# Two transformer blocks on one core: where the row sums of the conditioning products are issued, which engine does half of a norm's first pass, the root's steps, and when a norm's parameters are loaded

## The chip, the core and the metric

The kernel runs on one core of a Trainium2 chip. The engines of a core work side by side, each on a queue of its own in order: TensorE (PE in the profile, with PEld for its weight loads), VectorE (DVE), ScalarE (ACT), GpSimd (POOL) and SyncE (SP), whose queue issues nearly all DMA transfers. They wait for one another by semaphores. The metric is the device time of one execution in microseconds (us); lower is better.

## What is computed

256 tokens of width 1024 pass through a first block of two layers (with a memory of 256 tokens) and then through a second block of two layers, whose norms are modulated by a conditioning vector. Cut to what matters here:

```python
def layer_norm(x, g, b):
    xf = x.astype(jnp.float32)
    mu = jnp.mean(xf, axis=-1, keepdims=True)
    var = jnp.mean(jnp.square(xf - mu), axis=-1, keepdims=True)
    y = (xf - mu) * lax.rsqrt(var + LN_EPS) * g.astype(jnp.float32) + b.astype(jnp.float32)
    return y.astype(x.dtype)
...
    for l in range(DEPTH):
        x = layer_norm(DN_ALPHA * x + 0.5 * swiglu_ffn(x, ffn_w_in[l, 0], ffn_w_out[l, 0]),
                       ln_g[l, 0], ln_b[l, 0])
        x = layer_norm(DN_ALPHA * x + mixer_sublayer(x, w_mix_in[l], b_gate[l], kv_norm_g[l], w_uk[l],
...
        x = layer_norm(DN_ALPHA * x + memory_cross_attention(x, mem, xa_wq[l], xa_wkv[l], xa_wo[l]),
                       ln_g[l, 2], ln_b[l, 2])
        x = layer_norm(DN_ALPHA * x + 0.5 * swiglu_ffn(x, ffn_w_in[l, 1], ffn_w_out[l, 1]),
                       ln_g[l, 3], ln_b[l, 3])
...
def rms_norm_2(x, g):
    xf = x.astype(jnp.float32)
    y = xf * lax.rsqrt(jnp.mean(xf * xf, axis=-1, keepdims=True) + EPS)
    return (y * g.astype(jnp.float32)).astype(x.dtype)
...
def adaln(cond, mod_w, mod_b):
    return jnp.split(jax.nn.silu(cond) @ mod_w + mod_b, 6, axis=-1)

def modulate(h, shift, scale):
    return h * (1 + scale) + shift
```

The second block's layers add a gated mixer (even: two kinds of attention with a context stream beside the tokens; odd: neighbourhood attention) and a gated swiglu with d_ff 2816. Shift, scale and gate, six vectors of 1024 for each layer, come from `adaln`.

## The kernel before

**Matrix products.** Weights are loaded in fp32 as tiles of 128 x 1024 (`wf`, three buffers, 512 KB each) by SP. Each is split into a high part `wh` by a cast on ACT (L199) and a low part `wl` by a subtraction on DVE (L200); the activations are split in the same way. A product is then three matmuls on PE, L204 to L206. This fills PE for nearly the whole span, with DVE and ACT feeding it.

**The ends of stages.** The first block has four stages in each layer: `ffn_in` and `ffn_out`, `mixer`, `cross`, and a second pair `ffn_in` and `ffn_out`. Each ends in `post_ln`, which calls `layer_norm` for each half of the tokens (tb 0 and 1): L295 adds the accumulators from PSUM to the residual with its row sum, ACT squares, L302 gives the negated mean `nm`, L305 does the first pass (subtract the mean, multiply by g) on the first 512 columns and L313 on the second 512, L308 gives the variance `ve`, `rsqrt` (L248 to L260) the inverse root, and L314 does the last pass (multiply by the root, add b) on each half. Then PE transposes the result (L277) and the next stage begins. Its parameters g and b are two tiles of 512 KB, loaded by `ln_params` in `post_ln`, behind the loads of the stage in front. The kernel has eight such ends, and 16 calls of `layer_norm`.

**The root.** `rsqrt` begins with an integer operation on the bits (L248) and takes three Newton steps. For one value per partition (n = 1) a step has two operations, L256 and L260. For n > 1 there are ten in all. The second block's norms call it too (`modulating`, whose scaled activations are L970, and the norms of heads).

**The conditioning products.** `adaln` is a generator. It computes shift, scale and gate as 160 row sums on DVE (L911, a multiplication of a `wa` tile of 128 x 1024 with the conditioning vector, with accumulation). A `wa` tile has 512 KB and one buffer; the load of the next one is issued behind the last product that reads it. For layer 0 and the first two kinds of layer 1 a tile serves two products, for the other four kinds of layer 1 one. Whoever calls `mods(n)` pulls n products: the units of `ffn_in` from the third on (in the very first `ffn_in` from the eleventh on), and each unit of `ffn_out`. `until(thirds)` pulls all that are missing for a third of a layer's kinds: it stands behind the even attention (3), behind the `ffn_in` of the second block's first layer (4) and behind the odd attention (6), ahead of the output projection and of `gated`.

**The end of the odd attention.** The last heads' maxima (L462, L463), the splits of the output (L200), then the projection by `w2_out` (`projS`), `gated` (L1000 multiplies the accumulators by the gate, L1001 adds the residual), then the norm ahead of the last ffn (L964, L965, `rsqrt`, L970), whose transposes are PE's next work.

**What sets the order.** A scheduler of the framework orders each engine's instructions when the program is built, from the order of the code and the buffers; `self.held` keeps the first weight splits of the next stage behind the norm's last pass.

Of the kernel before, what the change touches and what calls it, by code (L numbers as in the profile page):

```python
# [25 lines left out]
FT = DFF // P  # L26
# [10 lines left out]
RSQRT_SCALE = 2.0 ** (-13 / 27)  # L37
RSQRT_SEED = 1597463007.0 + round(-13 / 27 * 2 ** 23) - 2.0 ** 31
# [67 lines left out]
class Net:  # L106
# [136 lines left out]
    def rsqrt(self, v, n):  # L243
# [9 lines left out]
        for i in range(3):  # L253
            a = self.t([P, 32], "ra", 2)[:, :n]
            if n == 1:
                V.scalar_tensor_tensor(a, y, v, y, ALU.mult, ALU.mult)  # L256
            else:
                V.tensor_tensor(a, y, z, ALU.mult)
            y2 = self.t([P, 32], "rq", 6)[:, :n]
            V.scalar_tensor_tensor(y2, a, 3 * s * s, y, ALU.subtract, ALU.mult)  # L260
            if n > 1 and i < 2:
                z2 = self.t([P, 32], "rq", 6)[:, :n]
                V.scalar_tensor_tensor(z2, a, 3 * s * s, z, ALU.subtract, ALU.mult)
                z = z2
            y = y2
            s = 2 * s ** 3
# [14 lines left out]
    def layer_norm(self, x, tb, acc, scale, gb, eps, xs, after):  # L281
# [23 lines left out]
        V.scalar_tensor_tensor(y[:, halves[0]], r[:, halves[0]], nm, gb[0][:, halves[0]], ALU.add, ALU.mult)  # L305
        jk = self.t([P, 3], "jd", 2)
# [4 lines left out]
        for i, s in enumerate(halves):  # L311
            if i == 1:
                V.scalar_tensor_tensor(y[:, s], r[:, s], nm, gb[0][:, s], ALU.add, ALU.mult)  # L313
# [29 lines left out]
    def post_ln(self, acc, x, scale, l, i, eps, want_xs=True):  # L343

        gb = self.ln_params(l, i)
# [9 lines left out]
    def ffn_in(self, src, streams, between=None):  # L355
# [20 lines left out]
        for j in range(2, FT):  # L376
            w = self.weight(src[j], UNIT)
            if not between or j > 9:
                self.mods(n)
# [28 lines left out]
    def projB(self, src, n, nk, part, amid=iter(()), done=()):  # L408
# [6 lines left out]
        for u in range(nu):  # L415
# [3 lines left out]
            if nk == FT:  # L419
# [409 lines left out]
    def first_block(self, dbg=None, depth=DEPTH):  # L829
# [19 lines left out]
        for l in range(depth):  # L849
            g = self.ffn_in(I["ffn_w_inA"][l, 0], [xs], between if l == 0 else None)  # L850
            if l == 0:
                self.constants()
                x = [self.k4() for _ in range(NT)]
                for tb in range(NT):
                    self.load(x[tb], I["xN"][:, tb])
            (acc,) = self.ffn_out(I["ffn_w_outB"][l, 0], 1, g)
            xs = self.post_ln(acc, x, 2 * ALPHA, l, 0, 4 * LN_EPS)
            if dbg: dbg(f"x{l}0", x)
            acc = self.mixer(l, xs)
            self.mem_kv(l)  # L860
            xs = self.post_ln(acc, x, ALPHA, l, 1, LN_EPS)
            if dbg: dbg(f"x{l}1", x)
            acc = self.cross(l, xs)
            xs = self.post_ln(acc, x, ALPHA, l, 2, LN_EPS)
            if dbg: dbg(f"x{l}2", x)
            g = self.ffn_in(I["ffn_w_inA"][l, 1], [xs])
            (acc,) = self.ffn_out(I["ffn_w_outB"][l, 1], 1, g, self.second_params() if l == DEPTH - 1 else iter(()))
            xs = self.post_ln(acc, x, 2 * ALPHA, l, 3, 4 * LN_EPS, want_xs=l < DEPTH - 1)
# [748 lines left out]
```

## Time and profile before

| | before |
|---|---|
| median of 3 runs | 2552.11 us (2548.66 to 2557.58) |
| the profiled execution | 2549.47 us, of which the span is 2547.7 |
| granted clock of TensorE, mean | 0.984 |
| PE busy | 96% of the span |
| DVE busy | 65% |
| ACT busy | 46% |
| GpSimd busy | 3% |
| products L911 | 160, 193.6 us |

A page gives each engine's busy time, the groups of instructions with their mean duration, and the idle time of an engine with what ended it. In a timeline row the first number is the start, the second the time the instruction (or a run of x such) took, and the brackets hold the idle time before it and what ended that. A tile's name stands for its class of buffers: `k` are the working tiles, `pa` and `pj` the PSUM accumulators, `wf`, `wh`, `wl` the weights, `wa` the conditioning weights.

### The profile page before, as it was taken

Reading aid. Unit: us, or ns where it says so; the run is one execution under the profiler, and the core shown is the slowest. Engines: PE = TensorE matmul, PEld = TensorE weight load, DVE = VectorE, ACT = ScalarE, POOL = GpSimd, SP = SyncE. Lnnn points to the kernel's source line nnn. Section 1 sums busy time; section 2 is a strip of 40 time slices with the busy share of each in tenths; the row PEclk is TensorE's granted clock in tenths of the full one; section 3 lists DMA queues with packets and bytes.
Section 4 is the critical chain, followed back from the end, with each engine's and each line's share of the span. In section 5 each row is a group of like instructions: output and inputs, shape, how many; then the busy total and the mean of one; then the engine's idle time right before and its main releaser. Section 6 shows DMA issues by size and latency. Waiting matters only on the chain.

```text
span 2547.7 us, 39416 instructions
## 1 busy us (share of the span) xinstructions
PE 2442.3 (96%) x15166; PEld 2138.6 (84%) x15166; DVE 1660.2 (65%) x3325; ACT 1177.6 (46%) x1948; POOL 68.7 (3%) x88
## 2 busy tenths in 40 slices
PE   8998999989999999999899999899999999998999
PEld 8987989869979979999789877677888887776997
DVE  6566776577667667766677776776554537646654
ACT  5444464454444444555444545654222324555542
POOL 0000100000000000100000000000000000032000
PEclk9999999999999999999999999999999999999999
DMA  7774535547757755446447642013455632342554
GB/s 260 232 245 163 163 116 184 184 140 242 243 178 249 235 188 179 142 143 208 167 170 241 226 161 70 31 42 109 158 188 192 214 102 91 110 99 74 182 191 140
DMA packets 138844, 423.64 MB, mean 166 GB/s; under 512 B 29128, under 2 KB 36000, under 8 KB 138528
## 3 DMA queue, kind: packets, MB, share of 16 engines
q1 hardware_dynamic: 138656, 421.12, 50.8%
q8 instruction: 119, 1.95, 0.3%
q14 instruction: 69, 0.57, 0.1%
HBM read 416.84 MB, written 4.23 MB: 165 GB/s over the span
## 4 chain that ended last, share of the span: by engine, by line
PE 77%; DVE 12%; DMA 5%; ACT 3%; issue 2%; POOL 0%; SPq 0%; POOLq 0%; ACTq 0%; DVEq 0%
PE pj L204 17%; PE pj L206 17%; PE pj L205 17%; PE pa L205 7%; PE pa L204 7%; PE pa L206 6%; DVE wl L200 3%; PE pa L277 3%; DMA k<-in_rpbF_dram 1%; DMA wf<-in_ffn_w_outB_dram 1%; DVE mx L462 1%; ACT wh L199 1%; DVE k L200 1%; ACT a L465 1%; DMA wf<-in_mix_A_dram 1%
## 5 line engine op out<-in xcount | busy, mean ns | idle before, releaser
L199 ACT CAST wh<-wf 128x1024 fp32r<-128x1024 f32 (+2 forms) x652 | 673.0, 1034 | 938.5 <-PE pj L205 232.0
L200 DVE TENSOR_TENSOR wl<-wf,wh 128x1024 fp32r<-128x1024 f32 (+2 forms) x652 | 783.8, 1207 | 452.7 <-PE pj L206 130.4
L204 PE MATMUL pj<-k,wh 128*128 128x256 f32 (+1 forms) x2896 | 841.6, 291 | 0.0
L205 PE MATMUL pj<-k,wh 128*128 128x256 f32 (+1 forms) x2896 | 838.6, 290 | 0.0
L206 PE MATMUL pj<-k,wl 128*128 128x256 f32 (+1 forms) x2896 | 838.4, 290 | 0.0
L204 PEld LDWEIGHTS pj<-k,wh 128*128 128x128 f32 x2896 | 554.6, 192 | 14.4 <-issue 7.1
L205 PEld LDWEIGHTS pj<-k,wh 128*128 128x128 f32 x2896 | 554.3, 191 | 8.5 <-issue 1.3
L206 PEld LDWEIGHTS pj<-k,wl 128*128 128x128 f32 x2896 | 554.3, 191 | 7.5 <-issue 0.7
L204 PE MATMUL pa<-wh,k 128*128 128x512 f32 x688 | 272.3, 396 | 2.4 <-ACT k L199 2.4
L205 PE MATMUL pa<-wl,k 128*128 128x512 f32 x688 | 274.2, 398 | 0.4 <-DVE wl L200 0.2
L204 PE MATMUL pj<-wh,k 128*128 128x512 f32 (+1 forms) x616 | 250.2, 408 | 12.5 <-ACT wh L199 7.3
L205 PE MATMUL pj<-wl,k 128*128 128x512 f32 (+1 forms) x616 | 249.6, 405 | 3.1 <-DVE wl L200 2.9
L911 DVE SCALAR_TENSOR_TENSOR k<-wa,cond 128x1024 bf16<-128x1024 f32 x160 | 193.6, 1222 | 83.5 <-DMA wa<-in_mod_wT_dram 83.2
L206 PE MATMUL pa<-wh,a 128*128 128x512 f32 x560 | 218.0, 390 | 0.0
L206 PE MATMUL pj<-wh,k 128*128 128x512 f32 (+1 forms) x496 | 199.8, 403 | 2.9 <-DVE k L200 2.9
L204 PEld LDWEIGHTS pa<-wh,k 128*128 128x128 f32 x688 | 129.0, 187 | 36.2 <-ACT k L199 3.5
L204 PEld LDWEIGHTS pj<-wh,k 128*128 128x128 f32 x616 | 119.8, 194 | 40.2 <-ACT wh L199 8.5
L205 PEld LDWEIGHTS pa<-wl,k 128*128 128x128 f32 x688 | 129.2, 188 | 28.7 <-DVE wl L200 1.2
L205 PEld LDWEIGHTS pj<-wl,k 128*128 128x128 f32 x616 | 120.0, 195 | 28.8 <-DVE wl L200 5.1
L277 PE MATMUL pa<-ident,k 128*128 128x128 f32 x580 | 96.5, 299 | 49.3 <-DVE k L314 23.1
L277 PEld LDWEIGHTS pa<-ident,k 128*128 128x128 f32 x580 | 70.7, 152 | 82.5 <-DVE k L314 29.5
L206 PEld LDWEIGHTS pa<-wh,a 128*128 128x128 f32 x560 | 105.4, 188 | 25.3 <-DVE a L200 0.5
(252 smaller groups left out, 2417.4 us busy)
## 6 DMA issues: line engine op xcount, KB each, us to landing
wf<-in_ffn_w_inA_dram SPq DMA_DIRECT2D x262, 512.0 KB, 4.3
wf<-in_ffn_w_outB_dram SPq DMA_DIRECT2D x132, 512.0 KB, 4.4
wf<-in_mix_A_dram SPq DMA_DIRECT2D x108, 512.0 KB, 3.7
wa<-in_mod_wT_dram SPq DMA_DIRECT2D x96, 512.0 KB, 4.3
wf<-in_w_branchA_dram SPq DMA_DIRECT2D x32, 384.0 KB, 3.1
wf<-in_od_w_dram SPq DMA_DIRECT2D x24, 512.0 KB, 3.9
wf<-in_w_mix_outB_dram SPq DMA_DIRECT2D x16, 512.0 KB, 4.7
wf<-in_w_outB_dram SPq DMA_DIRECT2D x16, 512.0 KB, 3.7
```

The lines of the kernel that those rows point to most:

```text
L199: self.nc.scalar.copy(h, x)
L200: self.nc.vector.tensor_tensor(l, x, h.bitcast(F32), ALU.subtract)
L204: mm(ps, sh, mh, start=start, stop=False)
L205: mm(ps, sh, ml, start=False, stop=False)
L206: mm(ps, sl, mh, start=False, stop=stop)
L277: self.nc.tensor.transpose(ps[:, i * P:(i + 1) * P], b, self.ident)
L462: V.reduce_max(mx[:, i:i + 1], ps[:, a:b], axis=AX.X)
L465: nc.scalar.activation(p[:, a:b], ps[:, a:b], AF.Exp, bias=mx[:, i:i + 1], scale=scale, accum_out=sm[:, i:i + 1])
L911: V.scalar_tensor_tensor(junk, w, 1.0, self.cond[:, s], ALU.mult, ALU.mult, accum_out=mod[:, n, s:s + 1])
```

## The change

`ffn_in` pulls products from its sixth unit on (`j > 4`) where it was the third, the very first one as before; `ffn_out` no longer pulls in its last three units. The first pass of the second 512 columns moves from DVE (one scalar_tensor_tensor, L313) to GpSimd (a tensor_scalar and a tensor_tensor). The root takes two steps, the first of a higher order and with an operation more, from another first guess: five operations behind the integer one for n = 1 where there were six. `ln_params` is called ahead of `ffn_out`, of `mem_kv` and of `cross`, and its tiles are handed to `post_ln`. In the changed program lines move: L200 is L201, L305 is L310, L314 is L319, L256 is L257, L260 is L265, L911 is L919, L1000 is L1008; L262 is the new operation of the root's first step.

```diff
@@ -34,8 +34,9 @@
 IDX_SCALE = float(8 ** -0.5 * 64 ** -0.5)
 UNIT = 2048
 
-RSQRT_SCALE = 2.0 ** (-13 / 27)
-RSQRT_SEED = 1597463007.0 + round(-13 / 27 * 2 ** 23) - 2.0 ** 31
+
+RSQRT_SCALE = -(3 / 8 * 2 ** (-1 / 3)) ** (1 / 5)
+RSQRT_SEED = 1597463007.0 + round(math.log2(-RSQRT_SCALE) * 2 ** 23) - 2.0 ** 31
 
 
 class Split:
@@ -250,20 +251,24 @@
         if n > 1:
             z = self.t([P, 32], "rq", 6)[:, :n]
             V.tensor_tensor(z, y, v, ALU.mult)
-        for i in range(3):
+        for i in range(2):
             a = self.t([P, 32], "ra", 2)[:, :n]
             if n == 1:
                 V.scalar_tensor_tensor(a, y, v, y, ALU.mult, ALU.mult)
             else:
                 V.tensor_tensor(a, y, z, ALU.mult)
+            c = -3 * s * s
+            if i == 0:
+                V.scalar_tensor_tensor(a, a, -10 / 3 * s * s, a, ALU.add, ALU.mult)
+                c = 5 * s ** 4
             y2 = self.t([P, 32], "rq", 6)[:, :n]
-            V.scalar_tensor_tensor(y2, a, 3 * s * s, y, ALU.subtract, ALU.mult)
-            if n > 1 and i < 2:
+            V.scalar_tensor_tensor(y2, a, c, y, ALU.add, ALU.mult)
+            if n > 1 and i == 0:
                 z2 = self.t([P, 32], "rq", 6)[:, :n]
-                V.scalar_tensor_tensor(z2, a, 3 * s * s, z, ALU.subtract, ALU.mult)
+                V.scalar_tensor_tensor(z2, a, c, z, ALU.add, ALU.mult)
                 z = z2
             y = y2
-            s = 2 * s ** 3
+            s = 8 / 3 * s ** 5
         return y
 
     def warm(self, func, src):
@@ -303,14 +308,14 @@
         V.tensor_tensor(far, nm, near, ALU.subtract)
         V.scalar_tensor_tensor(ss[:, 2:3], far, -float(D), far, ALU.mult, ALU.mult)
         V.scalar_tensor_tensor(y[:, halves[0]], r[:, halves[0]], nm, gb[0][:, halves[0]], ALU.add, ALU.mult)
+        nc.gpsimd.tensor_scalar(y[:, halves[1]], r[:, halves[1]], nm, 1.0, ALU.add, ALU.mult)
+        nc.gpsimd.tensor_tensor(y[:, halves[1]], y[:, halves[1]], gb[0][:, halves[1]], ALU.mult)
         jk = self.t([P, 3], "jd", 2)
         ve = self.t([P, 1], "ve", 2)
         V.tensor_scalar(jk, ss, 1.0 / D, eps, ALU.mult, ALU.add, accum_out=ve)
         rs = self.rsqrt(ve, 1)
         c = slice(tb * P, (tb + 1) * P)
         for i, s in enumerate(halves):
-            if i == 1:
-                V.scalar_tensor_tensor(y[:, s], r[:, s], nm, gb[0][:, s], ALU.add, ALU.mult)
             z = V.scalar_tensor_tensor(y[:, s], y[:, s], rs, gb[1][:, s], ALU.mult, ALU.add)
             if xs is not None:
                 ps = self.transposes([y[:, (4 * i + k) * P:(4 * i + k + 1) * P] for k in range(4)])
@@ -340,9 +345,8 @@
             self.load(gb[j], self.I[nm][l, i:i + 1, :].broadcast_to((P, D)))
         return gb
 
-    def post_ln(self, acc, x, scale, l, i, eps, want_xs=True):
-
-        gb = self.ln_params(l, i)
+    def post_ln(self, acc, x, scale, gb, eps, want_xs=True):
+
         xs = Split(self, KT) if want_xs else None
         z, zs = None, []
         for tb in range(NT):
@@ -375,7 +379,7 @@
             nc.scalar.copy(at(s, 0)[:, :, tb * P:(tb + 1) * P], pt[:, :256].rearrange("p (j t) -> p j t", j=2))
         for j in range(2, FT):
             w = self.weight(src[j], UNIT)
-            if not between or j > 9:
+            if j > (9 if between else 4):
                 self.mods(n)
             if j % (4 // n) == 0:
                 more()
@@ -416,7 +420,7 @@
             w = self.weight(src[u], UNIT)
             now = [part(i, u) for i in range(n)]
             next(amid, None)
-            if nk == FT:
+            if nk == FT and u < nu - 3:
                 self.mods(n)
             for i in range(n):
                 unit = (*now[i], w)
@@ -853,19 +857,23 @@
                 x = [self.k4() for _ in range(NT)]
                 for tb in range(NT):
                     self.load(x[tb], I["xN"][:, tb])
+            gb = self.ln_params(l, 0)
             (acc,) = self.ffn_out(I["ffn_w_outB"][l, 0], 1, g)
-            xs = self.post_ln(acc, x, 2 * ALPHA, l, 0, 4 * LN_EPS)
+            xs = self.post_ln(acc, x, 2 * ALPHA, gb, 4 * LN_EPS)
             if dbg: dbg(f"x{l}0", x)
             acc = self.mixer(l, xs)
+            gb = self.ln_params(l, 1)
             self.mem_kv(l)
-            xs = self.post_ln(acc, x, ALPHA, l, 1, LN_EPS)
+            xs = self.post_ln(acc, x, ALPHA, gb, LN_EPS)
             if dbg: dbg(f"x{l}1", x)
+            gb = self.ln_params(l, 2)
             acc = self.cross(l, xs)
-            xs = self.post_ln(acc, x, ALPHA, l, 2, LN_EPS)
+            xs = self.post_ln(acc, x, ALPHA, gb, LN_EPS)
             if dbg: dbg(f"x{l}2", x)
             g = self.ffn_in(I["ffn_w_inA"][l, 1], [xs])
+            gb = self.ln_params(l, 3)
             (acc,) = self.ffn_out(I["ffn_w_outB"][l, 1], 1, g, self.second_params() if l == DEPTH - 1 else iter(()))
-            xs = self.post_ln(acc, x, 2 * ALPHA, l, 3, 4 * LN_EPS, want_xs=l < DEPTH - 1)
+            xs = self.post_ln(acc, x, 2 * ALPHA, gb, 4 * LN_EPS, want_xs=l < DEPTH - 1)
             if dbg: dbg(f"x{l}3", x)
         return x
 
```

**Place 1, DVE at the end of the odd attention of the second block.** The rows before, from the last splits of the attention's output (`k` from `pa`) over the low parts of the output projection's weights to the gate:

```order
L200 TENSOR_TENSOR k_4566_22546<-pa_23307,k_4564_22544 128x256
L200 TENSOR_TENSOR k_4566_22546<-pa_23354,k_4564_22544 128x256
L200 TENSOR_TENSOR wl_23464<-wf_23461,wh_23463 128x1024
L200 TENSOR_TENSOR wl_23470<-wf_23467,wh_23469 128x1024
L200 TENSOR_TENSOR wl_23476<-wf_23473,wh_23475 128x1024
L200 TENSOR_TENSOR wl_23637<-wf_23634,wh_23636 128x1024
L1000 TENSOR_TENSOR k_4815_23529<-pa_23379,k_4814_23527 128x512
L1001 TENSOR_TENSOR k_4102_20485<-k_4102_20485,k_4815_23529 128x512
```

The rows now at the same place, up to the gate (L1008 was L1000; six products stand further up, most of them beside the last heads):

```order
L201 TENSOR_TENSOR wl_23238<-wf_23235,wh_23237 128x1024
L201 TENSOR_TENSOR wl_23393<-wf_23390,wh_23392 128x1024
L919 SCALAR_TENSOR_TENSOR k_4609_23098,mod_18996<-wa_23094,cond 128x1024
L919 SCALAR_TENSOR_TENSOR k_4611_23102,mod_18996<-wa_23100,cond 128x1024
L201 TENSOR_TENSOR wl_23399<-wf_23396,wh_23398 128x1024
L919 SCALAR_TENSOR_TENSOR k_4613_23106,mod_18996<-wa_23104,cond 128x1024
L919 SCALAR_TENSOR_TENSOR k_4615_23110,mod_18996<-wa_23108,cond 128x1024
L919 SCALAR_TENSOR_TENSOR k_4617_23114,mod_18996<-wa_23112,cond 128x1024
L919 SCALAR_TENSOR_TENSOR k_4619_23118,mod_18996<-wa_23116,cond 128x1024
L919 SCALAR_TENSOR_TENSOR k_4621_23122,mod_18996<-wa_23120,cond 128x1024
L919 SCALAR_TENSOR_TENSOR k_4623_23126,mod_18996<-wa_23124,cond 128x1024
L1008 TENSOR_TENSOR k_4657_23291<-pa_23141,k_4656_23289 128x512
```

The products of layer 1's last kinds, which had been issued long before, stand between the weights' splits and directly ahead of the gate. Here `wl_23238` is the last split of the output projection's weights, `wl_23393` and `wl_23399` belong to the ffn behind it.

**Place 2, DVE in the first `post_ln`, first half of the tokens.** The rows before, from the mean to the last pass:

```order
L305 SCALAR_TENSOR_TENSOR k_350_2063<-k_216_1523,nm_2074,k_326_2005 128x512
L304 SCALAR_TENSOR_TENSOR ss_2065<-nm_2074 128x1
L313 SCALAR_TENSOR_TENSOR k_350_2063<-k_216_1523,nm_2074,k_326_2005 128x512
L308 TENSOR_SCALAR jd_2079,ve_2080<-ss_2065 128x3
L248 TENSOR_SCALAR rq_2082<-ve_2080 128x1
L256 SCALAR_TENSOR_TENSOR ra_2084<-rq_2082,ve_2080 128x1
L260 SCALAR_TENSOR_TENSOR rq_2086<-ra_2084,rq_2082 128x1
L256 SCALAR_TENSOR_TENSOR ra_2088<-rq_2086,ve_2080 128x1
L260 SCALAR_TENSOR_TENSOR rq_2090<-ra_2088,rq_2086 128x1
L256 SCALAR_TENSOR_TENSOR ra_2092<-rq_2090,ve_2080 128x1
L260 SCALAR_TENSOR_TENSOR rq_2094<-ra_2092,rq_2090 128x1
L314 SCALAR_TENSOR_TENSOR k_350_2063<-k_350_2063,rq_2094,k_327_2006 128x512 x2
```

The rows now:

```order
L310 SCALAR_TENSOR_TENSOR k_343_2051<-k_216_1523,nm_2062,k_217_1526 128x512
L309 SCALAR_TENSOR_TENSOR ss_2053<-nm_2062 128x1
L201 TENSOR_TENSOR wl_2121<-wf_2118,wh_2120 128x1024
L315 TENSOR_SCALAR jd_2069,ve_2070<-ss_2053 128x3
L249 TENSOR_SCALAR rq_2072<-ve_2070 128x1
L257 SCALAR_TENSOR_TENSOR ra_2074<-rq_2072,ve_2070 128x1
L262 SCALAR_TENSOR_TENSOR ra_2074<-ra_2074 128x1
L265 SCALAR_TENSOR_TENSOR rq_2077<-ra_2074,rq_2072 128x1
L257 SCALAR_TENSOR_TENSOR ra_2079<-rq_2077,ve_2070 128x1
L265 SCALAR_TENSOR_TENSOR rq_2081<-ra_2079,rq_2077 128x1
L319 SCALAR_TENSOR_TENSOR k_343_2051<-k_343_2051,rq_2081,k_218_1527 128x512 x2
```

L313 is gone from DVE, the root is one operation shorter, with the square (L262) in its first step, and L310 reads a parameter tile of a lower number.

**Place 3, SP around the end of the first layer's mixer.** The rows before, at the norm's parameters (`xa_q` and `xa_woB` are weights of `cross`):

```order
L159 DMA wf_5567<-in_xa_q_dram 128x1024
L159 DMA wf_5573<-in_xa_q_dram 128x1024
L159 DMA wf_5579<-in_xa_q_dram 128x1024
L159 DMA wf_5711<-in_xa_woB_dram 128x1024
L159 DMA k_961_5451<-in_ln_g_dram 128x1024
L159 DMA k_962_5452<-in_ln_b_dram 128x1024
L159 DMA wf_5717<-in_xa_woB_dram 128x1024
L159 DMA wf_5723<-in_xa_woB_dram 128x1024
```

The rows now, at the same parameters, among the weights of the mixer's output projection:

```order
L160 DMA wf_5008<-in_w_branchA_dram 128x768
L160 DMA wf_5014<-in_w_branchA_dram 128x768
L160 DMA wf_5074<-in_w_mix_outB_dram 128x1024
L160 DMA k_913_5218<-in_ln_g_dram 128x1024
L160 DMA wf_5080<-in_w_mix_outB_dram 128x1024
L160 DMA wf_5110<-in_w_mix_outB_dram 128x1024
L160 DMA k_914_5219<-in_ln_b_dram 128x1024
L160 DMA wf_5116<-in_w_mix_outB_dram 128x1024
L160 DMA wf_5146<-in_w_mix_outB_dram 128x1024
```

The load of g moved from place 212 of SP's queue to place 187, that of b from 213 to 190.

## Rows read from the trace of the kernel before

**Rows 1.** The page's first section: busy us, share, instructions of each engine.

```profile
PE 2442.3 (96%) x15166; PEld 2138.6 (84%) x15166; DVE 1660.2 (65%) x3325; ACT 1177.6 (46%) x1948; POOL 68.7 (3%) x88
```

**Rows 2.** PE's waits: us in total, times, longest.

```profile
PE pa L277 <- DVE k L314: 23.1, 12, 4.5
PE pa L277 <- DVE k L970: 9.7, 3, 3.9
```

**Rows 3.** DVE's waits, the same columns.

```profile
DVE k L305 <- DMA k<-in_ln_g_dram: 13.7, 2, 8.0
```

**Rows 4.** Timeline of DVE and PE at both mixers' ends.

```profile
503.12 0.75 DVE L305 SCALAR_TENSOR_TENSOR k<-k,nm,k 128x512 f32<-128x512 f32 x1 [8.00 <-DMA k<-in_ln_g_dram]
...
505.29 1.97 PE L277 MATMUL pa<-ident,k 128*128 128x128 f32 x8 [4.46 <-DVE k L314]
515.54 1.71 PE L277 MATMUL pa<-ident,k 128*128 128x128 f32 x11 [1.23 <-DVE k L314]
...
1243.48 1.78 PE L277 MATMUL pa<-ident,k 128*128 128x128 f32 x8 [2.13 <-DVE k L314]
1253.54 0.66 PE L277 MATMUL pa<-ident,k 128*128 128x128 f32 x4 [1.70 <-DVE k L314]
```

**Rows 5.** Timeline of the first norm on DVE; two later stage ends on PE.

```profile
199.59 0.22 DVE L256 SCALAR_TENSOR_TENSOR ra<-rq,ve 128x1 f32<-128x1 f32 x1
199.84 0.16 DVE L260 SCALAR_TENSOR_TENSOR rq<-ra,rq 128x1 f32<-128x1 f32 x1
200.03 0.22 DVE L256 SCALAR_TENSOR_TENSOR ra<-rq,ve 128x1 f32<-128x1 f32 x1
200.17 1.22 DVE L200 TENSOR_TENSOR wl<-wf,wh 128x1024 fp32r<-128x1024 f32 x1
...
201.94 1.41 DVE L314 SCALAR_TENSOR_TENSOR k<-k,rq,k 128x512 f32<-128x512 f32 x2
...
757.99 1.69 PE L277 MATMUL pa<-ident,k 128*128 128x128 f32 x10 [3.45 <-DVE k L314]
1500.32 1.94 PE L277 MATMUL pa<-ident,k 128*128 128x128 f32 x8 [3.92 <-DVE k L970]
```

**Rows 6.** Timeline of GpSimd in two stretches, with one split of DVE.

```profile
273.32 1.49 POOL L656 TENSOR_TENSOR a<-k,sc 128x128 f32<-128x128 f32 x1
275.47 0.46 POOL L656 TENSOR_TENSOR a<-k,sc 128x128 f32<-128x128 f32 x1
...
273.27 1.23 DVE L200 TENSOR_TENSOR wl<-wf,wh 128x1024 fp32r<-128x1024 f32 x1 [0.51 <-issue]
...
2281.49 0.69 POOL L1362 TENSOR_SCALAR k<-k,sm 128x512 f32<-128x512 f32 x1
2282.15 1.00 POOL L1341 TENSOR_TENSOR k<-k,a 128x384 f32<-128x384 f32 x1
```

**Rows 7.** The products: all 160, two in a row, SP's issues, landing.

```profile
L911 DVE SCALAR_TENSOR_TENSOR k<-wa,cond x160: 1214/1222/1230, 26.5 to 2027.2; 128x1024 bf16<-128x1024 f32 x160
...
1988.34 1.22 DVE L911 SCALAR_TENSOR_TENSOR k<-wa,cond 128x1024 bf16<-128x1024 f32 x1 [1.27 <-DMA wa<-in_mod_wT_dram]
1993.14 1.22 DVE L911 SCALAR_TENSOR_TENSOR k<-wa,cond 128x1024 bf16<-128x1024 f32 x1 [1.25 <-DMA wa<-in_mod_wT_dram]
...
1989.60 0.33 SPq L159 DMA_DIRECT2D wa<-in_mod_wT_dram  x1
...
wa<-in_mod_wT_dram SPq DMA_DIRECT2D x96, 512.0 KB, 4.3
```

**Rows 8.** Timeline around the end of the odd attention.

```profile
2305.10 0.27 DVE L463 TENSOR_SCALAR mx<-mx 128x1 f32<-128x1 f32 x2
...
2335.34 0.69 DVE L1000 TENSOR_TENSOR k<-pa,k 128x512 f32<-128x512 f32 x1 [1.67 <-PE pa L206]
...
2345.56 0.88 DVE L970 TENSOR_SCALAR k<-k,rq 128x512 f32<-128x512 f32 x2
2346.20 1.17 PE L277 MATMUL pa<-ident,k 128*128 128x128 f32 x6 [2.73 <-DVE k L970]
```

## The prediction

> **What bounds the kernel now.** I read the busy times first: PE works 2442 of 2547.7 us [rows 1], so the other engines cost time only where PE stands still, and a change of this kind is worth what it does to PE's waits. Second, PE's waits by releaser [rows 2]. Those that the edits reach first: 23.1 us in 12 waits for L314, the last pass of a layer norm, and 9.7 us for L970, the scaled activations of the second block. Together 32.8 us, 1.3% of the span; nothing in the diff removes a matmul. Third, DVE's wait for a norm's parameters: 13.7 us in 2 waits [rows 3]. Fourth, the timeline at the ends of stages [rows 4, 5]: there PE has nothing else to do, and each DVE operation of the norm's chain is on the path. Fifth, the row sums of L911 ("products", 160 of them): 1.22 us each, the last one at 2027.2, before the odd mixer of the second block begins [rows 7]. They are all done where PE has other work, so today they are cover, not path.
>
> **Part 1, products moved.** The generator that issues a product at each `next` is pulled in fewer places: ffn_in units 2 to 4 and the last three units of each ffn_out no longer pull. Counting the pulls by the new conditions: in the first block 116 become 95; with those of the second block 146 of 160 are out before the odd mixer, where before all 160 were. The call `until(6)` after the odd mixer pulls what is left: 14 products, and for layer 1's last kinds each has a `wa` tile of its own. The order of DVE (place 1 above) shows them: they start beside the last heads of the odd attention and fill the row of DVE up to the last one, directly ahead of the first gated operation (L1000, now L1008), which must follow it on the engine. What is queued behind is the gate, the squares, the root and L970, and PE waits for L970.
>
> The price of one product is the cycle of the single `wa` buffer: product (1.22), the next load issued at once (1988.34 + 1.22 gives 1989.56, the issue stands at 1989.60), landing, next product. The nearest row has 1988.34 to 1993.14, 4.8 us; with the median landing of 4.3 the cycle is 5.5 [rows 7]. The first product can start at the maximum of the second last heads, about 2305.4 [rows 8]. The last ends at 2305.4 + 1.2 + 13 x 4.8 = 2369.0 at the least, 2378.1 at 5.5; I take 2373, nearer the cycle that was seen back to back. Before, the first gated operation ran at 2335.34 and L970 at 2345.56 [rows 8], paced by PE's own last matmuls. Behind a pile nothing paces them but DVE: eight passes of 0.69 for the gate and about 1.3 for the root, 6.8 us; the 10.2 of before is the other end. So L970 comes at 2373 + 6.8 = 2379.8 instead of 2345.6: **+34 us**, bounds +30 (2369.0 + 6.8) and +43 (2378.1 + 10.2). No other work covers it: PE ended the output projection at 2343.5 and stood still for 2.73 us before 2346.20 already [rows 8]; the next stage needs the whole row of activations. It would cost nothing below a cycle of (2335.3 - 2306.6) / 13 = 2.2 us, less than half of any seen.
>
> What the move gives back: at the ends of stages DVE no longer has a product of 1.22 us in front of the norm. The order shows that wl splits stand in their place, so I count this with the norms below, not as a term. `until(3)` ahead of the even output projection has two products more on one loaded tile, 2 x 1.22 = 2.4 us of DVE; PE has attention work beside most of it: **+1**, bounds 0 and +2.5.
>
> **Part 2, norm parameters earlier.** At the end of the mixer of each layer DVE waits for ln_g, 8.0 and 5.7 us [rows 3, 4]: their loads stood on SP's queue behind all the weights of the memory's keys, values and queries. SP's order (place 3 above) now has ln_g 25 places earlier, among the first weights of the mixer's output; the price is two 512 KB loads ahead of the rest of these weights and of the memory's (the memory's tiles go back some four places), and two of the twenty k4 tiles held longer, and I count it at nothing because the loads that it delays are those that ran ahead of their use while ln_g waited. PE's gaps at these two stage ends are 4.46 + 1.23 and 2.13 + 1.70 = 9.5 us [rows 4]. When ln_g is there, the chain runs right behind the accumulators, whose own wait takes part of the gap, but the second token half moves up too. I take **-9.5**; bounds -13.7 (the whole of DVE's wait) and 0 (the load is still late).
>
> **Part 3, GpSimd pass and shorter root at the norms.** Of the 23.1 us, 13.6 are left for the other stage ends, and the last of the first block adds 3.92 of L970's; 17.5 at most. Per token half the chain loses one pass of 128x512 (half of 1.41, 0.70) and of the root one step less one operation: a step of two takes 0.44 (199.59 to 200.03), the third operation of the new one about 0.22, so 0.2 [rows 5]. That is 0.9 per half, for twelve halves 10.9 us of DVE; but in the first example a wl split of 1.22 stands in the middle of the root's chain, and the 3.45 at 757.99 [rows 5] is made of such neighbours, which stay. Against it stands the work on GpSimd: a tensor_scalar of 0.69 and a tensor_tensor that by 1.00 for 384 columns is 1.3 for 512 [rows 6]: 2.0 us from the mean on, against 0.7 + 0.2 + 1.1 + 0.7 = 2.7 on DVE up to the second half's last pass. It fits by 0.7 if nothing disturbs it.
>
> What may disturb it is in the trace: the same 128x128 multiply on GpSimd took 0.46 alone and 1.49 when a wl split of DVE ran beside it (273.27 to 274.50) [rows 6], so one is held for the length of the other. The Trainium skill (SBUF — State Buffer, § Who interferes with whom) says that a DVE instruction with two SBUF inputs contends with a GpSimd instruction that reads SBUF, and that the one that is first holds the shared pair for the whole of its instruction. This speaks against the change, since both of the norm's remaining passes (L305, L314) and the wl splits have two SBUF inputs; by the rule alone the stage ends get worse and the sum is 2579, rival B; the trace's 1.49 agrees with it. In the sum, one operation held (1.49 - 0.46 = 1.0) in two halves of three takes 0.7 of the 0.9 per half, and 12 x 0.2 = 2.4 is left, with the head start of the wl splits a little more: I take **-4** for the stage ends; bounds -17.5 (all gaps gone) and +7 (each of the twelve halves held for 1.5, one operation for 1.0 and the other for half of that, and 0.9 saved).
>
> **Part 4, the root elsewhere.** In the second block the same root is used with one value or with many; a call of one saves 0.2, one of many two operations of ten, about 0.4. It stands ahead of PE in the 9.7 us for L970 [rows 2] and in front of the heads' attention. With some fifteen calls on the path, 0.2 each: **-3**; bounds -6 (0.4 each) and 0 (all hidden).
>
> **The sum** against the profiled execution's 2549.5 us (span 2547.7, 1.8 around it; the median of the three runs is 2552.1, 2.6 higher, so I stay on the lower side): 2549.5 + 34 + 1 - 9.5 - 4 - 3 = **2568.0 us**.
>
> **Rivals.**
> **A, the pile costs nothing:** the loads of the products run ahead of them, or the products find room in the odd attention. For it: DVE has idle time there, 1.67 us before 2335.34 alone [rows 8]. Against it: each load was issued only after its buffer's reader [rows 7], and thirteen cycles have 29 us. Then 2549.5 + 1 - 9.5 - 4 - 3 = 2534: faster. It decides from a cycle below 2.2 us.
> **B, GpSimd and DVE block each other at each norm:** the stage ends cost +7 in place of -4. For it: 0.46 became 1.49 [rows 6]. Against it: only some of the splits run at that moment. 2549.5 + 34 + 1 - 9.5 + 7 - 3 = 2579: slower.
> **C, not slower, the gaps of the stage ends close:** if L314 was late because products and its own pass stood in the row, all 17.5 us go and the root brings its 6: 2549.5 + 34 + 1 - 9.5 - 17.5 - 6 = 2551.5, no change. For it: PE's gaps there have no other cause in the rows than DVE. Against it: gaps of 2 us are hardly below the time from the last accumulator to the first transposed block, sum, mean, root and pass, of which 0.9 goes. It decides when more than 1.4 us of PE's wait go per half.
>
> **How the numbers follow.** Forecast (the pile costs 30 to 43, the norms give little): 0.71, by itself 2558 to 2577. B 0.13, C 0.11, A 0.05. A measurement of this kernel can tell about 0.3%, 7.7 us. Faster comes from A alone, 0.05; same from C, 0.11; slower from the forecast and B, 0.84. The range is 2556 to 2582: its upper end takes in B and the pile's longer cycle, its lower end the shortest cycle with half of the gaps closed; A and most of C lie outside.
>
> **What the changed kernel's profile would show.** Right: the products in a row between about 2305 and 2375, each waiting for `wa`, PE idle for some 30 us there and L1008 waiting for no matmul; DVE's wait for ln_g gone; at the stage ends PE's waits for L319 shorter by a few us in all; two GpSimd operations a norm half, some of them longer than 0.7 and 1.3. Wrong: a cycle of 3 us or less; products spread before 2305; gaps at the stage ends at zero (C), or longer than 2 us everywhere with GpSimd's operations at 2 us and more (B); an ln_g that still ends DVE's wait.

## The result and the profile after

The changed kernel takes **2572.4 us** (median of 6 runs, 2567.9 to 2575.5) where the kernel before takes 2549.2 (6 runs): a ratio of 1.0085, interval 1.0070 to 1.0101. It is slower by 23 us, where 18.5 had been forecast (2568.0 against the profiled 2549.5). Its profiled execution took 2574.6, of which the span is 2572.9.

The busy times answer to [rows 1]: PE works as long as before, DVE and ACT do not work longer, GpSimd does.

```profile
PE 2444.7 (95%) x15166; PEld 2138.5 (83%) x15166; DVE 1650.9 (64%) x3211; ACT 1176.7 (46%) x1948; POOL 112.2 (4%) x120
```

PE's waits after (in total, times, longest), against [rows 2]:

```profile
PE pj L949 <- DVE mod L927: 28.8, 1, 28.8
PE pa L282 <- DVE k L978: 12.2, 4, 5.8
PE pa L282 <- DVE k L319: 6.9, 6, 2.4
```

The wait for the norms' last pass fell from 23.1 to 6.9, and DVE's wait for ln_g [rows 3] is gone. In their place stands one wait of 28.8 us that did not exist: PE waits to transpose a modulation vector that the last product completes. Setting the two traces beside each other matmul by matmul (both have 15166 on PE), the changed kernel leads by 4.6 us at 600, 5.8 at 890, 11.4 at 1380, 11.7 at 1955 and 13.9 at 2278. From there to 2398 it loses 39.1, and it ends 25.2 behind: 3.4 of it while the products stand among the last heads and the output projection (up to 2332), 32.0 over the pause, and 3.7 behind it. The timeline of that stretch, the products on DVE, then PE (some products between are left out):

```profile
2291.20 1.22 DVE L919 SCALAR_TENSOR_TENSOR k<-wa,cond 128x1024 bf16<-128x1024 f32 x1
...
2345.00 1.23 DVE L919 SCALAR_TENSOR_TENSOR k<-wa,cond 128x1024 bf16<-128x1024 f32 x1 [3.59 <-DMA wa<-in_mod_wT_dram]
...
2359.57 1.23 DVE L919 SCALAR_TENSOR_TENSOR k<-wa,cond 128x1024 bf16<-128x1024 f32 x1 [3.65 <-DMA wa<-in_mod_wT_dram]
...
2360.72 0.69 DVE L1008 TENSOR_TENSOR k<-pa,k 128x512 f32<-128x512 f32 x1
...
2367.06 0.88 DVE L978 TENSOR_SCALAR k<-k,rq 128x512 f32<-128x512 f32 x2
...
2361.53 0.38 PE L949 MATMUL pj<-ident,mod 128*8 128x128 f32 x1 [28.77 <-DVE mod L927]
2367.69 1.94 PE L282 MATMUL pa<-ident,k 128*128 128x128 f32 x8 [5.78 <-DVE k L978]
```

Fourteen products stand in 2291.20 to 2360.8. They come every 5.3 us in the mean, and at the end every 4.8 to 4.9 us, of which 3.5 to 3.7 is waiting for the tile. The gate follows in the same tenth of a microsecond as the last one, and waits for no matmul. In [rows 8] it began at 2335.34 and waited for PE.

The next rows show TensorE's clock over the pause and behind it, in windows (columns: length, then busy time and count of PE, PEld, DVE, ACT, POOL, granted clock, DMA share, GB/s), first after, then before behind the same norm:

```profile
2333.00:2361.50 28.50, 0.00 (x0) 0.00 (x0) 8.10 (x15) 1.04 (x1) 0.00 (x0) 0.56 0.39 127
2361.50:2377.40 15.90, 7.54 (x21) 5.74 (x22) 12.95 (x33) 6.36 (x12) 0.00 (x0) 0.50 0.22 66
```

```profile
2346.60:2356.80 10.20, 7.32 (x22) 5.44 (x20) 7.40 (x19) 5.73 (x10) 0.00 (x0) 0.50 0.34 103
```

With PE idle from 2332.8 the granted clock falls to one half (1.2 of 2.4 GHz) at 2336.5, and it stays there until 2377.4, 9.7 us into the work behind the norm. Before, with a pause of 2.7, it was at one half for 10.2 us of the same work. So this half clock is nothing that the change adds: from the first transpose of the norm's result (2367.69 now, 2346.20 before) to the thirteenth product matmul behind it PE takes 9.76 us in both. That matmul now, then before:

```profile
2377.45 0.39 PE L205 MATMUL pj<-wh,k 128*128 128x512 f32 x1
```

```profile
2355.96 0.63 PE L204 MATMUL pj<-wh,k 128*128 128x512 f32 x1
```

The 3.7 us are lost further on, in two steps. PE waits for the first gated product of the ffn (L377, which was L373), and then the clock falls to one half once more. First PE's wait for L373 in the whole trace of before, then the two steps in the changed kernel:

```profile
PE pa L277 <- DVE k L373: 0.6, 1, 0.6
```

```profile
2383.72 0.44 PE L282 MATMUL pa<-ident,k 128*128 128x128 f32 x2 [2.49 <-DVE k L377]
...
2384.20:2387.70 3.50, 3.50 (x10) 2.78 (x9) 2.07 (x3) 1.27 (x3) 0.00 (x0) 0.51 0.00 0
```

L377 is not late: it starts 16.2 us behind L978, where L373 started 17.1 behind L970. PE comes to it sooner, as in the changed order 32 of its instructions stand between the first product matmul and that transpose, where 46 stood before. The trace of e2 below has both steps too (a wait of 2.3 us, one half from 2393.0 to 2396.4).

### The profile page after: what moved, and what is told of

Same layout as the page of the kernel before. It is cut to its first block, busy times and chain, and to the rows that moved or that the text cites. A ratio compares the mean times of both kernels' runs of the same rounds, so it can differ in the third digit from the quotient of the medians.

```text
span 2572.9 us, 39343 instructions
## 1 busy us (share of the span) xinstructions
PE 2444.7 (95%) x15166; PEld 2138.5 (83%) x15166; DVE 1650.9 (64%) x3211; ACT 1176.7 (46%) x1948; POOL 112.2 (4%) x120
## 4 chain that ended last, share of the span: by engine, by line
PE 75%; DVE 13%; DMA 6%; ACT 4%; issue 2%; SPq 0%; POOL 0%; ACTq 0%; DVEq 0%; POOLq 0%
PE pj L205 16%; PE pj L206 16%; PE pj L207 16%; PE pa L206 6%; PE pa L205 6%; PE pa L207 6%; DVE wl L201 3%; PE pa L282 2%; DMA wa<-in_mod_wT_dram 2%; DVE mx L466 1%; DMA wf<-in_mix_A_dram 1%; DMA wf<-in_ffn_w_inA_dram 1%; DVE k L919 1%; ACT wh L200 1%; DMA k<-in_rpbF_dram 1%
## 5 line engine op out<-in xcount | busy, mean ns | idle before, releaser
L200 ACT CAST wh<-wf 128x1024 fp32r<-128x1024 f32 (+2 forms) x652 | 673.0, 1034 | 988.9 <-DMA wf<-in_ffn_w_inA_dram 228.9
L201 DVE TENSOR_TENSOR wl<-wf,wh 128x1024 fp32r<-128x1024 f32 (+2 forms) x652 | 784.1, 1207 | 490.6 <-PE pj L207 135.4
L919 DVE SCALAR_TENSOR_TENSOR k<-wa,cond 128x1024 bf16<-128x1024 f32 x160 | 193.1, 1224 | 104.2 <-DMA wa<-in_mod_wT_dram 104.2
```

What stands on the lines that cost most here:

```text
L200: self.nc.scalar.copy(h, x)
L201: self.nc.vector.tensor_tensor(l, x, h.bitcast(F32), ALU.subtract)
L919: V.scalar_tensor_tensor(junk, w, 1.0, self.cond[:, s], ALU.mult, ALU.mult, accum_out=mod[:, n, s:s + 1])
```

## The experiments

All runs are of five rounds against the kernel before on the same chip. Differences are from that kernel's median in the same sitting (2549.1 for e1 to e4, 2549.1 for e5 to e8, 2550.8 for e9 to e11, 2549.2 for the change).

| run | what it is | median, us | ratio, interval | difference |
|---|---|---|---|---|
| the change | all parts | 2572.4 | 1.0085 (1.0070 to 1.0101) | +23.2 |
| e1 | the change, pulls as before | 2532.4 | 0.9937 (0.9924 to 0.9949) | -16.7 |
| e2 | before, pulls as changed | 2588.9 | 1.0156 (1.0143 to 1.0170) | +39.9 |
| e3 | the change, the 14 in the odd projection | 2538.2 | 0.9956 (0.9943 to 0.9970) | -10.8 |
| e4 | the change, two wa tiles | 2560.4 | 1.0045 (1.0028 to 1.0062) | +11.4 |
| e5 | e1 without GpSimd | 2529.8 | 0.9929 (0.9913 to 0.9944) | -19.3 |
| e6 | e1, parameters late | 2546.5 | 0.9992 (0.9979 to 1.0005) | -2.6 |
| e7 | e1, old root | 2541.1 | 0.9970 (0.9957 to 0.9984) | -8.0 |
| e8 | the change, ten left behind | 2552.7 | 1.0016 (1.0007 to 1.0025) | +3.6 |
| e9 | before, parameters early alone | 2544.1 | 0.9977 (0.9967 to 0.9987) | -6.7 |
| e10 | before, the root alone | 2540.8 | 0.9958 (0.9943 to 0.9972) | -10.0 |
| e11 | e5, ends free, the 14 in the odd projection | 2532.8 | 0.9931 (0.9917 to 0.9945) | -18.0 |

**Where is the loss: e1 and e2.** The edit of e1 to the changed kernel; e2 is the other side of it, on the kernel before.

```diff
-            if j > (9 if between else 4):
+            if not between or j > 9:
                 self.mods(n)
...
-            if nk == FT and u < nu - 3:
+            if nk == FT:
                 self.mods(n)
```

> The changed kernel with the products pulled where they were before; the other three parts stay. Theory (the pile of 14 products behind the odd attention is the whole loss, about +39, and the other parts give the 13.9 us by which the changed trace leads at 2291): 2549 - 14 = 2535, ratio 0.9945, no PE wait of 28.8 us. Rival 1 (the other parts gain only because the products had left the ends of the stages): a product of 1.22 stands ahead of the norm again in most of the 16 halves, and only the parameters' 9 to 10 us are left: 2540 or more. Rival 2 (GpSimd and DVE blocking each other is a large part of the loss): 2555 or more.

> The kernel before with only the products' pulls changed; norms, root and parameters as before. Theory (the moved pulls cost 39 and give nothing back): 2549 + 39 = 2588, ratio 1.015. Rival 1 (the ends of the stages gain by being free of products): 4 to 10 us less, 2578 to 2584. Rival 2 (the loss lies in the other parts): 2560 or less.

Measured: -16.7 and +39.9. Both theories hold within 3 us, and the parts add up: 39.9 - 16.7 = 23.2, the whole change. In e2's trace the long wait is there again, and PE's wait for the last pass at the ends of the stages has not shrunk (24.8 against 23.1):

```profile
PE pj L941 <- DVE mod L919: 28.5, 1, 28.5
PE pa L277 <- DVE k L314: 24.8, 12, 4.4
```

In e1's the wait of L949 is not among those listed, and L319's is nearly as short as in the whole change, with the products where they always were:

```profile
PE pa L282 <- DVE k L978: 9.1, 4, 3.4
PE pa L282 <- DVE k L319: 8.7, 7, 1.9
```

So the slowdown is the moved pulls. What the move was to free is hardly there to be had: where the pile begins, e2's trace is 1.4 us ahead of the trace of before (at 2278), and the changed kernel's is 1.2 ahead of e1's.

**What makes a product dear: e3, e4, e8.** e3 pulls the 14 in the odd projection, one for each group of rows of its queries, keys and values:

```diff
+                    self.mods(1)
                     c = slice(tb * P, (tb + 1) * P)
...
             for s, tb, ps in self.groupB(I["od_w"][4 + u], 512, streams):
+                self.mods(1)
```

> The changed kernel whole, with one more pull for each of the 20 row groups of the odd projection, so that the 14 products that are left are issued there, one for each group of about 8 us, and none behind the odd attention. Theory (they cost only because they stand in a row where PE has nothing else): 2549 - 14 = 2535, ratio 0.9945, and faster than both kernels. Rival (a product costs wherever the split of the weights queues behind its wait for wa): each takes 1 to 4 us of the odd projection, 14 to 50 in all: 2549 to 2580.

Measured -10.8: the 39 are gone, and the kernel is faster than the one before. It is not e1, though: 5.9 us more by the medians, where a difference of two runs is uncertain by 4 to 5. Beside e1's trace e3's leads by 6.4 us at 2065 and by 3.0 at 2185, so about 3.3 are lost in the odd projection, where most of these products stand. That is the rival in small: a quarter of a microsecond each, not one to four. (These are single executions, e1's the slowest of its five and e3's the fastest: e3's ends 3.3 ahead there, against the medians.)

e8 has the call in the query part alone, four pulls, so that ten products stay behind the attention:

```diff
+                    if n == 0:
+                        self.mods(1)
                     c = slice(tb * P, (tb + 1) * P)
```

> The changed kernel with four pulls in the query part of the odd projection, so that ten products stand behind the odd attention in place of fourteen. Theory (first at about 2291, then one in each cycle of 4.9 of the one buffer; free as long as the last ends ahead of the first gated operation, 2325 in that frame): the last ends at 2291.4 + 1.2 + 9 x 4.9 = 2337, the norm's chain comes 9 to 12 late against the kernel with none left (2538): 2548. Rival (each product costs its share of the 39, 2.8): 2538 + 28 = 2566. Rival 2 (below a number near ten all is hidden): 2538.

Measured 2552.7, 4.7 above the forecast of 2548; 2566 by shares and 2538 by hiding are further off. Its trace, products and gate on DVE, then PE:

```profile
2287.84 1.22 DVE L919 SCALAR_TENSOR_TENSOR k<-wa,cond 128x1024 bf16<-128x1024 f32 x1
...
2337.46 1.23 DVE L919 SCALAR_TENSOR_TENSOR k<-wa,cond 128x1024 bf16<-128x1024 f32 x1 [4.52 <-DMA wa<-in_mod_wT_dram]
2338.61 0.69 DVE L1008 TENSOR_TENSOR k<-pa,k 128x512 f32<-128x512 f32 x1
...
2339.43 0.38 PE L949 MATMUL pj<-ident,mod 128*8 128x128 f32 x1 [10.69 <-DVE mod L927]
```

Nine cycles in 49.6 us, 5.5 each. PE's wait fell from 28.8 to 10.7, which is 4.5 us for each product that left. The price is then a chain of loads with a free stretch at its start. By the medians the change is 34.2 us above e3, which has no product left there, and 19.7 above e8, which has ten: 4.9 for each of the four that left. At this price 34.2 us are seven products. So seven or so cost nothing and each further one a cycle, by this estimate.

e4 gives the products a second tile, and takes a k4 tile for the room:

```diff
-                w = self.t([P, D], "wa", 1, pool=self.wp)
+                w = self.t([P, D], "wa", 2, pool=self.wp)
...
-        return self.t([P, 1024], "k4", 20, dt)
+        return self.t([P, 1024], "k4", 19, dt)
```

> The changed kernel with two wa buffers in place of one; to make room, 19 k4 tiles in place of 20. The products stay where the change put them. Theory (the price is the cycle of the one buffer, 4.9 us): with two loads under way a cycle is about (1.2 + 4.3) / 2 = 2.8, the last of 14 ends at about 2291 + 13 x 2.8 = 2328, ahead of PE's last accumulation at 2333, and the loss is gone but for a few us: 2535 to 2541. Rival 1 (the two loads share what the DMA queue moves, so that the cycle stays over 4): the last ends at 2345 to 2355 and 2555 to 2565. Rival 2 (it is the place in the row, not the load): 2572 as it is.

Measured +11.4. The 2560.4 lie in the range of rival 1, but not by its cause, a cycle that stays over 4. The trace has two effects of opposite sign. Behind the attention the cycle is now (2349.87 - 2308.94) / 13 = 3.1, forecast 2.8, PE's wait for L949 is 4.2 us where it was 28.8, and from 2295 to the end the kernel gains 25.4 on the whole change:

```profile
2308.94 1.21 DVE L919 SCALAR_TENSOR_TENSOR k<-wa,cond 128x1024 bf16<-128x1024 f32 x1
...
2349.87 1.23 DVE L919 SCALAR_TENSOR_TENSOR k<-wa,cond 128x1024 bf16<-128x1024 f32 x1 [2.47 <-DMA wa<-in_mod_wT_dram]
```

But it arrives there 17.4 late. The loss sits at ends of stages (PE waits 20.0 us for L319 in all, 6.9 in the whole change), of which the first after `cross` shows how (DVE, then PE):

```profile
554.30 1.21 DVE L919 SCALAR_TENSOR_TENSOR k<-wa,cond 128x1024 bf16<-128x1024 f32 x1
...
555.52 1.21 DVE L919 SCALAR_TENSOR_TENSOR k<-wa,cond 128x1024 bf16<-128x1024 f32 x1
...
556.85 1.23 DVE L919 SCALAR_TENSOR_TENSOR k<-wa,cond 128x1024 bf16<-128x1024 f32 x1
...
558.53 1.22 DVE L919 SCALAR_TENSOR_TENSOR k<-wa,cond 128x1024 bf16<-128x1024 f32 x1
...
560.22 1.23 DVE L919 SCALAR_TENSOR_TENSOR k<-wa,cond 128x1024 bf16<-128x1024 f32 x1
...
561.37 1.41 DVE L319 SCALAR_TENSOR_TENSOR k<-k,rq,k 128x512 f32<-128x512 f32 x2
...
562.17 2.40 PE L282 MATMUL pa<-ident,k 128*128 128x128 f32 x10 [6.17 <-DVE k L319]
```

The order that was built for these tile counts puts five products between the norm's variance, its root and its last pass, and PE waits 6.2 us for L319 where its longest wait in the whole change is 2.4. A product at the end of a stage can cost, then, when it stands inside the norm's chain. The run changes two pools at once; whether the second `wa` tile or the missing k4 tile led to this order, no run tells.

**The other parts: e5, e6, e7, e9, e10.** Each takes one part out of e1, or puts one alone into the kernel before. e5:

```diff
-        nc.gpsimd.tensor_scalar(y[:, halves[1]], r[:, halves[1]], nm, 1.0, ALU.add, ALU.mult)
-        nc.gpsimd.tensor_tensor(y[:, halves[1]], y[:, halves[1]], gb[0][:, halves[1]], ALU.mult)
...
         for i, s in enumerate(halves):
+            if i == 1:
+                V.scalar_tensor_tensor(y[:, s], r[:, s], nm, gb[0][:, s], ALU.add, ALU.mult)
```

> The kernel of e1_pulls_back with the second half's first pass back on DVE (one scalar_tensor_tensor); parameters early and the shorter root stay. Theory (GpSimd takes a pass of 0.75 from DVE but holds it up: in e1's trace L309 takes 0.52 where it took 0.15, L310 0.88 for 0.75, L262 0.36 for 0.16, together about 0.7 per half): no net effect, 2530 to 2535. Rival 1 (the pass on GpSimd is a gain of 0.75 in the 12 halves on the path, less a little): 2537 or more. Rival 2 (the lock is a net loss, since the second token half's chain grew from 5.1 to 7.0 in four places): 2528 or less.

e6 calls `ln_params` in `post_ln` again, at all four stages; e9 has the reverse of this edit on the kernel before.

```diff
-    def post_ln(self, acc, x, scale, gb, eps, want_xs=True):
+    def post_ln(self, acc, x, scale, l, i, eps, want_xs=True):
+
+        gb = self.ln_params(l, i)
...
-            gb = self.ln_params(l, 1)
             self.mem_kv(l)
-            xs = self.post_ln(acc, x, ALPHA, gb, LN_EPS)
+            xs = self.post_ln(acc, x, ALPHA, l, 1, LN_EPS)
```

e7 has the old root with its constants; e10 has the new one on the kernel before.

```diff
-        for i in range(2):
+        for i in range(3):
...
-            c = -3 * s * s
-            if i == 0:
-                V.scalar_tensor_tensor(a, a, -10 / 3 * s * s, a, ALU.add, ALU.mult)
-                c = 5 * s ** 4
...
-            s = 8 / 3 * s ** 5
+            s = 2 * s ** 3
```

> The kernel of e1_pulls_back with the norm parameters loaded in post_ln again, behind the loads of the stage in front. Theory (the early loads give PE's 9.5 us at the two mixers' ends): 2532.4 + 9.5 = 2542, with DVE's wait for ln_g back at about 13.7 us. Rival (half of it is lost again where the half clock falls and where the k4 tiles are held): 2536 to 2538.

> The kernel of e1_pulls_back with the root of three Newton steps and its old first guess. Theory (an operation saved in each of 30 calls with one value and two in 24 calls with eight, about fifteen on the path): 2532.4 + 3 = 2535.4. Rival 1 (all of it is hidden): 2532. Rival 2 (the second block's gains of 4 to 5 us are all the root's): 2537 or more.

> The kernel before with only the norm parameters loaded a stage earlier. Theory (the parameters are the largest of the gains, 14.1 by e6 against e1, more than PE's 9.5 us of gaps at the two mixers' ends, since half clock behind these gaps goes too): 2549 - 13 = 2536. Rival (the surplus over 9.5 is the scatter between chips): 2549 - 9.5 = 2539.5 or more.

> The kernel before with only the shorter root. Theory 1 (as predicted, 0.2 to 0.4 us for each of some fifteen calls on the path): 2549 - 3 to 5 = 2544 to 2546. Theory 2 (e7 against e1: 8.7): 2540. Rival (hidden): 2549.

Against these forecasts e5 came out at the lower edge of its theory and e10 at its second theory (2540). The others missed theirs: e6 came 4.5 above its theory, e7 is in the range of its second rival (2537 or more), and e9 in that of its rival (2539.5 or more), 8 above its theory. Each part has three pairs of runs, which share runs among them. An interval of 0.13% on a ratio makes a difference of two uncertain by some 4 to 5 us.

| part | pairs | differences, us | mean |
|---|---|---|---|
| early parameters | e9; e5 - e10; e1 - e6 | -6.7, -9.3, -14.1 | -10 |
| root | e10; e5 - e9; e1 - e7 | -10.0, -12.6, -8.7 | -10 |
| GpSimd | e1 - e5; e6 - e10; e7 - e9 | +2.6, +7.4, -1.4 | +3, not told from 0 |

In e6 the wait of [rows 3] is back:

```profile
DVE k L310 <- DMA k<-in_ln_g_dram: 13.3, 2, 7.4
```

The root's gain is spread over PE's waits. Two rows of before that were not shown above, then e10's four:

```profile
PE pa L277 <- DVE a L1141: 7.1, 4, 5.3
PE pa L277 <- DVE k L1016: 6.0, 6, 3.5
```

```profile
PE pa L282 <- DVE k L319: 17.9, 9, 3.2
PE pa L282 <- DVE k L976: 8.9, 4, 3.2
...
PE pa L282 <- DVE a L1147: 6.3, 4, 5.3
PE pa L282 <- DVE k L1022: 4.0, 4, 3.3
```

Together 45.9 before and 37.1 now: 8.8 us, most of it (5.2) at the ends of the first block's stages. Not all of it need be the root's: the wait for ln_g happens to be 2.0 shorter in this trace (11.7 against 13.7), and the execution (2536.6) is one of the fastest of its six.

**Are free ends worth anything: e11.** The pulls of e3 on the kernel of e5.

> The kernel of e5_no_gpsimd (2529.8) with the products away from the ends of the stages as in the change, the 14 that are left issued in the odd projection. Theory (freeing the ends gives less than the 14 products cost in the odd projection, as e3 against e1, +5.9): 2533 to 2536. Rival (with the first pass back on DVE an end that is free of products gives 4 or more): 2526 or less.

Measured 2532.8, at the lower edge of its theory: 3.0 above e5 by the medians and 1.3 by the differences from the kernel before, inside the uncertainty of the pair: no gain that can be told. In its trace it leads e5 by 5.0 at 1511 and is 2.0 behind at 2188, past most of the odd projection; of the lead I cannot say how much is the clock, whose half stretches add up to 62 us in the whole trace and to 73 in e5's. e5 is the fastest that was run, ahead of both kernels; e1 and e11 lie within its uncertainty.

## The prediction, point by point

**Part 1, the pile: right.** Forecast +34 (30 to 43), measured 39.9 (e2 against before, and again the change against e1). Nearly all of what the whole forecast lacked, 18.5 against 23.2, lies in this term. Its steps, with the 13.9 of the lead added to the changed trace's times: first product at 2305.1 (forecast 2305.4); last one's end at 2374.7 (2373); from there to L978 6.3 us (6.8); L978 35.4 late (34.2). The rest, 3.7 us, came behind it, a term that the sum did not have: the wait for L377 and the second stretch of half clock shown above. Place and cycle were read from [rows 7, 8]; the mean cycle was 5.3 where the 2373 stands for 5.1. e8 and e4 show the cycle as the cause: four products fewer take 18.1 us off PE's wait, and a second tile leaves 4.2 of 28.8, though the totals of both runs missed their forecasts. That the last products' transpose (L949) stands on PE's queue too, and takes most of the wait on itself, was not seen; it moved nothing, as L978 is late by the same chain.

**`until(3)`, +1:** not separated by any run.

**Part 2, -9.5: right in size.** Mean -10 over three pairs, and no ln_g wait is left in the changed trace; of PE's 9.5 us at the two mixers' ends 2.0 are left there (0.99 and 1.00). The pairs scatter from -6.7 to -14.1.

**Parts 3 and 4, -4 and -3: the sum fair, the division wrong.** Without the pulls the whole gain was forecast as 16.5 (9.5 + 4 + 3), and e1 measured 16.7. That it agrees so closely is luck: it is the root that gives 10, where some 2.4 in the norms and 3 elsewhere were reckoned, and GpSimd, from which only a small head start was expected, gives nothing that can be told (+3). The size that failed is the root's: I put fifteen calls on the path beside the norms. All 64 calls together save DVE 14 us of busy time (1660.2 to 1646.5 in e10), and up to 8.8 of it came off PE's waits, so as much as two thirds of the saving lay on the path; the trace also has less time at half clock (61 us in all in e10's, 82 in that of before), though single executions differ in that anyway. GpSimd: the hold that was forecast is there in size and place. Groups of the changed kernel (busy us, mean ns):

```profile
L312 POOL TENSOR_TENSOR k<-k,k 128x512 f32<-128x512 f32 x16 | 23.5, 1468 | 1.3
L1370 POOL TENSOR_SCALAR k<-k,sm 128x512 f32<-128x512 f32 x32 | 22.0, 695 | 15.4 <-DVE sm L471 8.9 <-PE pj L1361 3.7 <-DVE mx L467 2.5
L311 POOL TENSOR_SCALAR k<-k,nm 128x512 f32<-128x512 f32 x16 | 20.9, 1309 | 1193.9 <-DVE jc L307 643.4 <-DVE nm L308 286.0 <-DMA wf<-in_ev_lat_dram 188.5
...
L257 DVE SCALAR_TENSOR_TENSOR ra<-rq,ve 128x1 f32<-128x1 f32 x60 | 15.9, 265 | 1.9
L310 DVE SCALAR_TENSOR_TENSOR k<-k,nm,k 128x512 f32<-128x512 f32 x16 | 14.1, 879 | 0.0
...
L262 DVE SCALAR_TENSOR_TENSOR ra<-ra 128x1 f32<-128x1 f32 x30 | 10.7, 355 | 0.9
...
L309 DVE SCALAR_TENSOR_TENSOR ss<-nm 128x1 f32<-128x1 f32 x16 | 8.4, 522 | 0.1
```

and of e5, where GpSimd has no part in the norm:

```profile
L257 DVE SCALAR_TENSOR_TENSOR ra<-rq,ve 128x1 f32<-128x1 f32 x60 | 13.1, 218 | 1.6
...
L310 DVE SCALAR_TENSOR_TENSOR k<-k,nm,k 128x512 f32<-128x512 f32 x16 | 11.9, 745 | 0.0
...
L262 DVE SCALAR_TENSOR_TENSOR ra<-ra 128x1 f32<-128x1 f32 x30 | 4.8, 159 | 0.9
...
L309 DVE SCALAR_TENSOR_TENSOR ss<-nm 128x1 f32<-128x1 f32 x16 | 2.5, 153 | 0.1
```

A tensor_scalar of the same shape takes 0.70 on GpSimd at L1370 and 1.31 in the mean at L311. On DVE L310 takes 0.13 more, L262 0.20, L257 0.05, and L309, which computes 128 numbers, 0.52 where it takes 0.15 in e5. Two instances on GpSimd, one that no long operation of DVE stood beside (474.00) and one at the second half of the first norm, then the operation of DVE beside the latter:

```profile
474.00 0.70 POOL L311 TENSOR_SCALAR k<-k,nm 128x512 f32<-128x512 f32 x1 [140.86 <-DVE nm L308]
...
205.68 1.84 POOL L312 TENSOR_TENSOR k<-k,k 128x512 f32<-128x512 f32 x1
...
206.28 1.26 DVE L309 SCALAR_TENSOR_TENSOR ss<-nm 128x1 f32<-128x1 f32 x1
```

L309 ends at 207.54, with GpSimd's operation (207.52). Sixteen passes of 0.75 left DVE, 11.9 us; 2.2 + 5.9 + 5.9 + 2.8 = 16.8 came back in these four lines (L310, L262, L309, L257), and DVE as a whole works longer with the help of GpSimd than without it (1651.5 us in e1, 1645.5 in e5). The Trainium skill (SBUF — State Buffer, § Who interferes with whom) has this rule, that a DVE instruction with two SBUF inputs and a GpSimd instruction that reads SBUF exclude one another for the length of the whole instruction; the 1.26 us for 128 numbers agrees with it. Whether that makes a net loss, as rival B said, the three pairs do not tell.

**The rivals.** A fell with the first trace (a cycle of 4.8 and more, one load behind each reader). C fell with e1 and e2. It needs 33.0 us of gain beside the pile (9.5 + 17.5 + 6), and e1 has 16.7. Its reason, products in front of L314, fell with e2, which has the changed pulls and still waits 24.8 us for L314. B's mechanism is real and its price of +7 at the norms is at the edge of what the pairs leave open (mean +3).

## What to carry to other kernels

Work that is taken out of a busy stretch has to go somewhere, so count what the catch-all at the end still has to issue, and price it by its own chain (here one buffer, one load: 4.9 us for a product of 1.2), not by its engine time. A small serial chain that PE waits for some dozens of times, like a root of six operations of 0.2 us, can be worth more to shorten (here some 10 us) than a large operation is to move to an engine which then holds up the first (here no gain that can be told). Look at the built order for what stands inside such a chain: behind five products there, in e4, PE waits 6.2 us.

## What the runs showed of the chip

The granted clock fell to one half 3.7 us into the pause of 28.8 and stayed there for the first 9.7 us of the work behind it. A pause of 2.7 us in the kernel before was followed by half clock as well, and the same work took the same 9.76 us. So at the clock the long pause cost no more here than the short one. A 128x1 operation of DVE with two inputs took up to 1.26 us where it takes 0.15 alone, while a 128x512 operation ran on GpSimd.

The sum of half-clock stretches differs from one kernel's profiled execution to the next (55 us in e1's, 73 in e5's, of which e5 has the lower median), so that a shift of 3 to 5 us between two traces at some place in the middle is not evidence by itself; the medians of five or more runs were needed for each part.
